# The chunk inverses of a gated DeltaNet in two 16-row blocks instead of one 32-row loop

## The chip, the cores and the metric

The kernel runs on one core of one Trainium2 chip. The metric is the device time of one execution in microseconds (us). An engine's instructions run in the order that was fixed when the program was built: a scheduler places every instruction of TensorE (PE), VectorE (DVE), ScalarE (ACT), GpSimd (POOL) and the DMA queue of SyncE (SP) by a simulated timeline, and each engine then takes its own list from the top, waiting at each instruction for what it needs.

## The reference

Two layers of a hybrid encoder on 512 tokens of width 1024. A layer has a mixer (a gated MLP, a sliding-window attention and a bidirectional gated DeltaNet, each on its own columns of one projection), then 16 experts and an input gate. The part that matters here is the DeltaNet, cut from the reference:

```python
lower = jnp.where(strict, jnp.einsum('bhntd,bhnsd->bhnts', k_beta, kc) * decay, 0.0)
eye = jnp.eye(C, dtype=F32)
t_inv = lax.linalg.triangular_solve(lower + eye, jnp.broadcast_to(eye, lower.shape),
                                    left_side=True, lower=True, unit_diagonal=True)
u = t_inv @ (vc * bc[..., None])
w = t_inv @ (k_beta * jnp.exp(gc)[..., None])
...
def step(state, inp):
    v_new = u_n - w_n @ state
    o_n = (q_n * jnp.exp(g_n)[..., None]) @ state + qk_n @ v_new
    ...
o_f = gated_delta_chunked(q, k, v, g[0], beta[0])
o_b = flip(gated_delta_chunked(flip(q), flip(k), flip(v), flip(g[1]), flip(beta[1])))
```

For every head, chunk and direction, a unit lower triangular matrix has to be inverted before the scan over the chunks can start.

## The kernel before

The kernel cuts the tokens into 16 chunks of 32 (6 heads, 2 directions: 192 matrices of 32x32; on the tiles the four chunks of a token tile lie in the four groups of 32 partitions, with 24 matrices of each direction in the free dimension; the chunk length changes nothing in the result). A mixer runs in this order of code: the norm, the gated MLP, the decays, the DeltaNet's projections, `gdn_chunk` (the matrices `AT`, from the products pG, L867), `gdn_inv` (L875), the MLP's output, `attn_qk` (L464), `gdn_inv_T` (L897), and then the scan (`gdn_scan`, L907) with its fill work between the steps (the attention's values vp, its core, the first part of the output projection). The scheduler moves work of these parts past each other.

`gdn_inv` inverts on VectorE. AT is transposed so that each matrix lies within a partition (X, 1024 elements a direction), multiplied by minus the betas (L887), and then inverted in place by 30 steps of forward substitution; step j multiplies a column by a row (L892, into T) and adds the product (L894), both directions at once. `gdn_inv_T` transposes X back into XT (L903) and scales it by the betas (L904). The scan's first product, pV (L943, 12 products of 32x32 by 32x64 a step), reads XT.

`attn_qk` has three projection blocks (0, 1, 2) of 256 columns of queries and keys. For each it runs 96 products (name qkp, lines L340 to L342 of a helper: high by high, low by high, high by low), squares on ScalarE for the norms, a reciprocal square root by Newton steps on VectorE (L175 to L182, 13 small operations), a scaling on POOL (L522, four operations), the rotary products on VectorE (L527, four or eight, then L529 and L530), and transposes on TensorE (qkTp, L496), whose copies ScalarE makes (L501, L502, L504). The high halves of the weights are made by ScalarE (L330, whi) and the low halves by POOL (L332, wlo), 512 elements a piece for these blocks and 384 for the attention's values.

The transposes of a block and the copies of the block before are interleaved in the code: after each token tile of block i comes one tile of block i-1.

Tiles come from pools: `slot` has 12 buffers of 128x2048, `gslot` two (X and XT take them here), PSUM's `pg` four.

Of the kernel before, what the change touches and what calls it, by code (L numbers as in the profile page):

```python
# [14 lines left out]
AF = mybir.ActivationFunctionType  # L15
ALU = mybir.AluOpType
# [93 lines left out]
class K:  # L110
# [428 lines left out]
    def gmlp(self, l, w):  # L539
# [12 lines left out]
        for t in range(NT):  # L552
# [6 lines left out]
            v.scalar_tensor_tensor(uv[:, t, :], x2, 1.0, p, op0=ALU.add, op1=ALU.mult)  # L559
            v.tensor_reduce(mu[:, t, :], vv[:, t], axis=AX.X, op=ALU.add)  # L560
            v.tensor_scalar(mu[:, t, :], mu[:, t, :], 1.0 / 64, None, op0=ALU.mult)
            v.tensor_tensor(vv[:, t], vv[:, t], mu[:, t, :, None].to_broadcast([128, 4, 64]), op=ALU.subtract)
            sq = self.p1([128, 4, 64], "sqv")
            act.activation(sq, vv[:, t], AF.Square)
            v.tensor_reduce(var[:, t, :], sq, axis=AX.X, op=ALU.add)
        f = lambda a: a.rearrange("p t g -> p (t g)")
# [308 lines left out]
    def gdn_inv(self, l):  # L875
        self.mark("inv")
        nc, mp = self.nc, self.mp
        v, act, pe, pool_e = nc.vector, nc.scalar, nc.tensor, nc.gpsimd
        br, AT = self.br, self.AT
        brT = self.small([128, 2, 32], "brT")  # L880
        v.transpose(brT, br)
        v.tensor_scalar(brT, brT, -1.0, None, op0=ALU.mult)
        X = self.gslot("X").rearrange("p (c i j) -> p c i j", c=2, i=32)
        for dr in range(2):
            Xd = X[:, dr] if dr == 0 else X[:, dr].rearrange("p i j -> p j i")
            v.transpose(Xd, AT[:, dr].rearrange("p m b -> p b m"))
            v.tensor_tensor(Xd, Xd, brT[:, dr, :, None].to_broadcast([128, 32, 32]), op=ALU.mult)  # L887
        pool_e.memset(X.rearrange("p c i j -> p c (i j)")[:, :, ::33], 1.0)
        for j in range(1, 31):
            n = 31 - j  # L890
            T = self.t(3, [128, 2, n, j], "T")
            v.tensor_tensor(T, X[:, :, j + 1:, j:j + 1].to_broadcast([128, 2, n, j]),  # L892
                            X[:, :, j:j + 1, 0:j].to_broadcast([128, 2, n, j]), op=ALU.mult)
            v.tensor_tensor(X[:, :, j + 1:, 0:j], X[:, :, j + 1:, 0:j], T, op=ALU.add)  # L894
        self.X = X

    def gdn_inv_T(self, l):  # L897
        self.mark("invT")
        v, pe, br, X = self.nc.vector, self.nc.tensor, self.br, self.X
        XT = self.XT = self.gslot("XT").rearrange("p (d m b) -> p d m b", d=2, m=32)  # L900
        for dr in range(2):
            Xd = X[:, dr] if dr == 0 else X[:, dr].rearrange("p i j -> p j i")
            v.transpose(XT[:, dr].rearrange("p m t -> p t m"), Xd)  # L903
        v.tensor_tensor(XT[:, :, 0:24], XT[:, :, 0:24], br[:, :, 0:24, None].to_broadcast([128, 2, 24, 32]), op=ALU.mult)  # L904


    def gdn_scan(self, l):  # L907
        nc, mp = self.nc, self.mp
        v, act, pe, pool_e = nc.vector, nc.scalar, nc.tensor, nc.gpsimd
        KQT, XT, QKm, kdec, vtok, EG, DC = self.KQT, self.XT, self.QKm, self.kdec, self.vtok, self.EG, self.DC  # L910
        o_sum = self.o_sum = self.gslot("o_sum")[:, :NT * 384].rearrange("p (t n) -> p t n", t=NT)
# [3 lines left out]
        for n in range(NCH):  # L915
# [25 lines left out]
            for h in range(6):  # L941
                for dr, ch, cc, tl in cur:
                    pe.matmul(pV[kl[dr], h, :], XT[kl[dr], dr, 6 * tl + h, :],  # L943
                              rhs[dr][:, h * 64:(h + 1) * 64], start=True, stop=True)
# [552 lines left out]
```

## Time and profile before

| | us |
|---|---|
| median of 3 runs | 1959.53 (1959.13 to 1962.07) |
| the profiled execution | 1958.17 |
| its span, first to last instruction | 1956.2 |
| TensorE busy | 1799.0 (92%) |
| VectorE busy | 930.7 (48%) |
| ScalarE busy | 523.6 (27%) |
| POOL busy | 457.6 (23%) |

The profile is of one execution. Of its span, the inversion in the first layer runs from 168 to 228 us and in the second from some 1130 to 1192; the experts fill most of the rest. Times below are us from the start of the span. A float32 product of TensorE stands in the trace as two records, so a pV of 12 products is "x24". Busy time of TensorE counts overlapping products once.

### The profile page before, as it was taken

The page shows a single profiled execution, that of the slowest core. Times are in us where ns is not written, and L with a number is a line of the kernel's source. Part 1 is how long each engine was busy: PE and PEld are TensorE (multiplying, and loading weights), DVE is VectorE, ACT ScalarE, POOL GpSimd, SP SyncE. Part 2 cuts the span into 40 slices and gives each one's busy share as a digit, 9 for nine tenths or more (in the row PEclk, how much of TensorE's full clock was granted, in tenths as well). Part 3 has the DMA queues.
Part 4 walks back from the last instruction along what each step waited for, and adds up shares of the span by engine and source line. Part 5 has one row for each costly group of instructions (what it writes and reads, how often), then busy time and mean ns, then how long its engine had stood idle before and what let it go on. Part 6 is the DMA issues. An engine that isn't in the chain of part 4 may idle for free.

```text
span 1956.2 us, 30065 instructions
## 1 busy us (share of the span) xinstructions
PE 1799.0 (92%) x12216; PEld 1126.8 (58%) x12216; DVE 930.7 (48%) x2088; ACT 523.6 (27%) x1213; POOL 457.6 (23%) x402
## 2 busy tenths in 40 slices
PE   5898698979999999999988978899799999999998
PEld 5777665864434444335987767568544343443368
DVE  5879868661211111422788896786511212114135
ACT  4334444231111101102443344452211010011032
POOL 3544413420000003201645352233100000022033
PEclk9989889989999999999998978899799999999999
DMA  5212020287899999999242020204798999999981
GB/s 169 87 34 60 17 85 16 109 321 296 347 412 412 390 412 411 366 414 374 85 131 82 21 71 24 76 2 168 305 356 345 412 406 395 415 372 393 414 289 65
DMA packets 168730, 467.46 MB, mean 239 GB/s; under 512 B 11664, under 2 KB 68496, under 8 KB 168592
## 3 DMA queue, kind: packets, MB, share of 16 engines
q1 hardware_dynamic: 161504, 458.46, 61.0%
q10 hardware_dynamic: 7088, 7.09, 1.2%
q8 instruction: 96, 1.57, 0.3%
q14 instruction: 42, 0.34, 0.1%
HBM read 461.32 MB, written 4.19 MB: 238 GB/s over the span
## 4 chain that ended last, share of the span: by engine, by line
PE 68%; DVE 21%; ACT 4%; issue 3%; POOL 2%; DMA 2%; SPq 1%; ACTq 0%; DVEq 0%; POOLq 0%
PE pGt L1270 15%; PE pUp L1270 11%; PE pY L1270 10%; DVE acc L770 3%; PE xep L1198 2%; DVE rr L936 2%; PE ysc L1289 2%; PE xep L1199 2%; PE op L340 1%; PE ysc L1290 1%; PE pV L943 1%; PE plep L1164 1%; PE pgp L342 1%; PE pgp L340 1%; PE pY L1385 1%
## 5 line engine op out<-in xcount | busy, mean ns | idle before, releaser
L1270 PE MATMUL pUp<-w,xe 128*64 128x512 f32 x800 | 200.8, 595 | 0.0
L1270 PE MATMUL pGt<-w,xe 128*64 128x512 f32 x640 | 200.4, 600 | 0.0
L332 POOL TENSOR_TENSOR wlo<-w,whi 128x512 fp32r<-128x512 f32 (+5 forms) x66 | 161.3, 2463 | 114.7 <-ACT whi L330 99.9
L1270 PE MATMUL pY<-w,hidT 128*64 128x512 f32 x720 | 186.9, 596 | 0.0
L1337 POOL TENSOR_TENSOR x<-x,hh 128x1024 f32<-128x1024 f32 x8 | 18.9, 2358 | 615.5 <-DVE x L1295 615.4
L1270 PEld LDWEIGHTS pUp<-w,xe 128*64 128x64 f32 x800 | 70.7, 137 | 101.8 <-issue 98.0
L1295 DVE TENSOR_TENSOR x<-ysc,x 128x512 f32<-128x512 f32 x96 | 63.2, 686 | 117.9 <-PE ysc L1290 117.9
L1270 PEld LDWEIGHTS pGt<-w,xe 128*64 128x64 f32 x640 | 58.6, 136 | 99.7 <-issue 97.6
L1270 PEld LDWEIGHTS pY<-w,hidT 128*64 128x64 f32 x720 | 64.1, 136 | 89.9 <-issue 87.4
L1270 PE MATMUL pGt<-wx,xe 128*64 128x512 f32 x320 | 114.4, 603 | 0.3
L1328 DVE SCALAR_TENSOR_TENSOR hid<-sg,gsl,pUp 128x512 f32<-128x512 f32 x32 | 23.7, 747 | 159.7 <-PE pUp L1270 158.1
L1354 DVE SCALAR_TENSOR_TENSOR yl<-pY,gsl,yh 128x512 fp32r<-128x512 f32 x28 | 21.0, 751 | 165.2 <-ACT yh L1353 163.7
L1321 DVE SCALAR_TENSOR_TENSOR sg<-sg,pGt 128x512 f32<-128x512 f32 x32 | 21.8, 686 | 132.2 <-ACT sg L1320 132.2
L330 ACT ACTIVATE whi<-w 128x512 fp32r<-128x512 f32 (+5 forms) x66 | 68.0, 1058 | 38.5 <-PE op L341 15.8
L342 PE MATMUL pgp<-whi,gTl 128*128 128x256 f32 x256 | 72.8, 292 | 3.9 <-DVE gTl L271 3.9
L329 POOL TENSOR_TENSOR w<-w,pp 128x512 f32<-128x512 f32 x32 | 32.4, 1047 | 179.2 <-DMA w<-in_w_ple_gate_dram 107.7
L1320 ACT ACTIVATE sg<-pGt,gsl 128x512 f32<-128x512 f32 x32 | 21.8, 687 | 192.2 <-PE pGt L1270 190.2
L340 PE MATMUL pgp<-whi,gTh 128*128 128x256 f32 x256 | 73.0, 289 | 0.0
L1200 ACT ACTIVATE xe<-xep,pp 128x256 f32<-128x256 f32 x64 | 30.2, 474 | 158.7 <-PE xep L1199 158.7
L341 PE MATMUL pgp<-wlo,gTh 128*128 128x256 f32 x256 | 72.4, 288 | 0.0
L1198 PE MATMUL xep<-OH,hh 128*128 128x256 f32 x256 | 69.1, 304 | 2.5 <-DVE OH L1186 2.5
L1344 ACT ACTIVATE hidT<-htp 128x512 f32<-128x512 f32 x32 | 19.1, 597 | 193.5 <-PE htp L1343 193.5
(404 smaller groups left out, 4277.0 us busy)
## 6 DMA issues: line engine op xcount, KB each, us to landing
w<-in_w_e_up_dram SPq DMA_DIRECT2D x100, 1024.0 KB, 14.6
w<-in_w_e_down_dram SPq DMA_DIRECT2D x90, 1024.0 KB, 11.3
w<-in_w_e_gate_dram SPq DMA_DIRECT2D x80, 1024.0 KB, 12.9
wx<-in_w_e_gate_dram SPq DMA_DIRECT2D x40, 1024.0 KB, 11.6
wx<-in_w_e_up_dram SPq DMA_DIRECT2D x28, 1024.0 KB, 12.2
wx<-in_w_e_down_dram SPq DMA_DIRECT2D x22, 1024.0 KB, 8.3
wd<-in_w_e_down_dram SPq DMA_DIRECT2D x32, 512.0 KB, 8.8
w<-in_w_in_dram SPq DMA_DIRECT2D x14, 1024.0 KB, 5.0
```

What stands on the lines that cost most here:

```text
L330: self.nc.scalar.activation(rr_(hi[:, ks, :]), wk, AF.Copy)
L332: e.tensor_tensor(rr_(lo[:, ks, :]), wk, hi[:, ks, :], op=ALU.subtract)
L340: pe.matmul(p, lh, rh, start=first, stop=False)
L341: pe.matmul(p, lh, rl, start=False, stop=False)
L342: pe.matmul(p, ll, rh, start=False, stop=last)
L770: v.scalar_tensor_tensor(acc, raw[:, kk:kk + S], conv[:, b, kk:kk + 1], acc, op0=ALU.mult, op1=ALU.add)
L936: v.tensor_tensor(rr[kl[dr], :], vtok[kl[dr], tl, :], fl(tm[kl[dr]]), op=ALU.subtract)
L1198: pe.matmul(p, rr_(hh[:, t, ks]), OHf[:, t, :], start=(t == 0), stop=False)
L1199: pe.matmul(p, rr_(hl[:, t, ks]), OHf[:, t, :], start=False, stop=(t == NT - 1))
L1270: pe.matmul(pt[nh][64 * ei:64 * ei + 64, :], lhs[:, kk, 64 * ei:64 * ei + 64], wt[ei][k][:, nh * 512:nh * 512 + 512], start=(kk == 0), sto ...
L1289: pe.matmul(p, rr_(OT[:, t, :]), rr_(yh[:, ns]), start=True, stop=False)
L1295: v.tensor_tensor(xv, p, xv, op=ALU.add)
```

## The change

X keeps its place, but only its two 16x16 diagonal blocks are inverted by VectorE: they are taken into a buffer XN (four blocks: two directions by two), and a loop of 14 steps inverts all four at once. ScalarE copies the inverted blocks into X, whose other two quadrants POOL has set to zero. In `gdn_inv_T`, XN is then used again for X transposed the other way; TensorE multiplies the block of AT between the two diagonal blocks by one inverse (pY1), VectorE scales that by the betas into a buffer Y, TensorE multiplies it by the other inverse (pY2), and VectorE subtracts the result from XT and scales XT by the betas, each direction by itself. Each of pY1 and pY2 is 192 products of 32x32 by 32x16 a layer.

```diff
         X = self.gslot("X").rearrange("p (c i j) -> p c i j", c=2, i=32)
+        XN = self.XN = self.slot("XN")
+        B = XN[:, 0:1024].rearrange("p (c e i j) -> p c e i j", c=2, e=2, i=16)
         for dr in range(2):
             Xd = X[:, dr] if dr == 0 else X[:, dr].rearrange("p i j -> p j i")
             v.transpose(Xd, AT[:, dr].rearrange("p m b -> p b m"))
-            v.tensor_tensor(Xd, Xd, brT[:, dr, :, None].to_broadcast([128, 32, 32]), op=ALU.mult)
-        pool_e.memset(X.rearrange("p c i j -> p c (i j)")[:, :, ::33], 1.0)
-        for j in range(1, 31):
-            n = 31 - j
-            T = self.t(3, [128, 2, n, j], "T")
...
+            for i in range(2):
+                s = slice(16 * i, 16 * i + 16)
+                Bd = B[:, dr, i] if dr == 0 else B[:, dr, i].rearrange("p i j -> p j i")
+                v.tensor_tensor(Bd, Xd[:, s, s], brT[:, dr, s, None].to_broadcast([128, 16, 16]), op=ALU.mult)
+        Bf = B.rearrange("p c e i j -> p (c e) i j")
+        pool_e.memset(Bf.rearrange("p c i j -> p c (i j)")[:, :, ::17], 1.0)
+        pool_e.memset(X[:, :, 0:16, 16:32], 0.0)
+        pool_e.memset(X[:, :, 16:32, 0:16], 0.0)
+        for j in range(1, 15):
+            n = 15 - j
+            T = self.t(3, [128, 4, n, j], "T")
+            v.tensor_tensor(T, Bf[:, :, j + 1:, j:j + 1].to_broadcast([128, 4, n, j]),
+                            Bf[:, :, j:j + 1, 0:j].to_broadcast([128, 4, n, j]), op=ALU.mult)
+            v.tensor_tensor(Bf[:, :, j + 1:, 0:j], Bf[:, :, j + 1:, 0:j], T, op=ALU.add)
+        for i in range(2):
+            s = slice(16 * i, 16 * i + 16)
+            act.activation(X[:, :, s, s], B[:, :, i], AF.Copy)
...
         XT = self.XT = self.gslot("XT").rearrange("p (d m b) -> p d m b", d=2, m=32)
+        XN = self.XN.rearrange("p (d m b) -> p d m b", d=2, m=32)
+        Y = self.slot("Y").rearrange("p (d m b) -> p d m b", d=2, m=32)
+        cs = [(slice(0, 16), slice(16, 32)), (slice(16, 32), slice(0, 16))]
         for dr in range(2):
+            nc.gpsimd.memset(Y[:, dr, 0:24, cs[dr][1]], 0.0)
+        for dr in range(2):
+            v.transpose(flip(XN[:, dr]), flip(X[:, dr]) if dr == 0 else X[:, dr])
+        for dr in range(2):
+            p = self.pg([128, 24, 16], "pY1")
+            for m in range(24):
+                for r in rows:
+                    pe.matmul(p[r, m, :], AT[r, dr, m, :], XN[r, dr, m, cs[dr][0]], start=True, stop=True)
+            v.tensor_tensor(Y[:, dr, 0:24, cs[dr][0]], p, br[:, dr, 0:24, None].to_broadcast([128, 24, 16]), op=ALU.mult)
+        for dr in range(2):
+            v.transpose(flip(XT[:, dr]), X[:, dr] if dr == 0 else flip(X[:, dr]))
+        for dr in range(2):
+            p = self.pg([128, 24, 16], "pY2")
+            for m in range(24):
+                for r in rows:
+                    pe.matmul(p[r, m, :], Y[r, dr, m, :], XT[r, dr, m, cs[dr][1]], start=True, stop=True)
+            xo = XT[:, dr, 0:24, cs[dr][1]]
+            v.tensor_tensor(xo, xo, p, op=ALU.subtract)
+            xd = XT[:, dr, 0:24]
+            v.tensor_tensor(xd, xd, br[:, dr, 0:24, None].to_broadcast([128, 24, 32]), op=ALU.mult)
-            Xd = X[:, dr] if dr == 0 else X[:, dr].rearrange("p i j -> p j i")
-            v.transpose(XT[:, dr].rearrange("p m t -> p t m"), Xd)
-        v.tensor_tensor(XT[:, :, 0:24], XT[:, :, 0:24], br[:, :, 0:24, None].to_broadcast([128, 2, 24, 32]), op=ALU.mult)
```

In the changed kernel the lines are: the loop L901 and L903, ScalarE's copies L906, XN's transposes L924, pY1's products L929, Y's scaling L930, XT's transposes L932, pY2's products L937, the subtraction L939, the scaling L941, and pV L980. The lists below name the buffers of pY1 pY_2097 (first direction) and pY_2195 (second), and those of pY2 pY_2295 and pY_2394.

The lists of the engines change order as well, in both layers alike. On TensorE, in the changed kernel, the products qkp of block 1 are interrupted after 47 of its 96 (the rest of the 96 follow):

```order
L342 MATMUL qkp<-whi,xl 128x256
L340 MATMUL qkp<-whi,xh 128x256
L341 MATMUL qkp<-wlo,xh 128x256
L342 MATMUL qkp<-whi,xl 128x256
L929 MATMUL pY_2097<-XN,AT 32x16 x14
L340 MATMUL qkp<-whi,xh 128x256
L341 MATMUL qkp<-wlo,xh 128x256
L342 MATMUL qkp<-whi,xl 128x256
L340 MATMUL qkp<-whi,xh 128x256
```

Before, nothing stood between these products; now 14 of pY1 do, so what follows on TensorE waits for the first of XN's transposes. pY1 goes on in 12 more pieces through block 2, up to a last one of 87.

On TensorE at the first block's transposes, before (the products here belong to block 2):

```order
L340 MATMUL qkp<-whi,xh 128x256
L341 MATMUL qkp<-wlo,xh 128x256
L342 MATMUL qkp<-whi,xl 128x256
L496 MATMUL qkTp<-cst,qk 128x128 x4
L340 MATMUL qkp<-whi,xh 128x256
L341 MATMUL qkp<-wlo,xh 128x256
L342 MATMUL qkp<-whi,xl 128x256
L340 MATMUL qkp<-whi,xh 128x256
```

and in the changed kernel, where block 2's first product is the last L340 shown:

```order
L342 MATMUL qkp<-whi,xl 128x256
L340 MATMUL qkp<-whi,xh 128x256
L929 MATMUL pY_2097<-XN,AT 32x16 x14
L496 MATMUL qkTp<-cst,qk 128x128 x2
L929 MATMUL pY_2097<-XN,AT 32x16 x21
L496 MATMUL qkTp<-cst,qk 128x128 x2
L929 MATMUL pY_2097<-XN,AT 32x16 x6
L340 MATMUL qkp<-whi,xh 128x256
```

Here 41 products of pY1 stand in three pieces around four transposes, ahead of block 2's first product. Before, block 0's first transposes came behind block 2's 23rd product; now its first four stand 11 products ahead of block 1's end, and the others follow as shown.

On VectorE, the end of the inversion, before (L529 and L530 are block 1's, L175 is block 2's):

```order
L529 TENSOR_TENSOR qk<-ro 128x16x8
L530 TENSOR_TENSOR qk<-ro 128x16x8
L892 TENSOR_TENSOR T<-X 128x60
L894 TENSOR_TENSOR X<-X,T 128x2x30
L903 STREAM_TRANSPOSE XT<-X 128x32x32 x2
L904 TENSOR_TENSOR XT<-XT,br 128x2x768
L175 TENSOR_SCALAR nr<-ssq 128x16
```

and in the changed kernel (L175 to L182, L527 to L530 all of block 2):

```order
L930 TENSOR_TENSOR Y<-pY_2097,br 128x24x16
L175 TENSOR_SCALAR nr<-ssq 128x16
L930 TENSOR_TENSOR Y<-pY_2195,br 128x24x16
L176 TENSOR_SCALAR nr<-nr 128x16
L177 TENSOR_SCALAR nr<-nr 128x16
L932 STREAM_TRANSPOSE XT<-X 128x32x32 x2
...
L181 TENSOR_TENSOR nr<-nr 128x16
L182 SCALAR_TENSOR_TENSOR ra<-nr,ra 128x16
L939 TENSOR_TENSOR XT<-XT,pY_2295 128x24x16
L941 TENSOR_TENSOR XT<-XT,br 128x768
L527 TENSOR_TENSOR ro<-qk,rot 128x128 x4
L529 TENSOR_TENSOR qk<-ro 128x16x8
L530 TENSOR_TENSOR qk<-ro 128x16x8
L939 TENSOR_TENSOR XT<-XT,pY_2394 128x24x16
L941 TENSOR_TENSOR XT<-XT,br 128x768
```

L175 of block 2 moved ahead of the transposes into XT, and block 2's rotary (L527 to L530) ahead of the last subtraction and scaling of XT; before, it came behind pV.

On POOL, the changed kernel has the order: four low halves of block 1, block 0's scaling, four low halves of block 2, Y's two memsets, block 1's scaling, four low halves of the values, block 2's scaling, the last four low halves. Before, the eight low halves of blocks 1 and 2 came ahead of block 0's scaling, and block 2's scaling came last. On ScalarE, L906 stands behind the first high half of block 2, and the others behind L906. SP's order is unchanged. The second V weights' low half takes Y's slot, and so waits for pY2.

## Rows read from the trace of the kernel before

**Rows 1.** The page: busy time by engine, and the chain that ended last by engine.
```profile
PE 1799.0 (92%) x12216; PEld 1126.8 (58%) x12216; DVE 930.7 (48%) x2088; ACT 523.6 (27%) x1213; POOL 457.6 (23%) x402
...
PE 68%; DVE 21%; ACT 4%; issue 3%; POOL 2%; DMA 2%; SPq 1%; ACTq 0%; DVEq 0%; POOLq 0%
```

**Rows 2.** Windows: stretch, its us, busy us by engine, granted clock, DMA share, GB/s.
```profile
182.50:196.00 13.50, 12.88 (x107) 12.68 (x105) 13.40 (x26) 9.24 (x43) 7.00 (x5) 0.99 0.42 114
196.00:207.00 11.00, 0.55 (x5) 0.37 (x4) 10.39 (x17) 0.33 (x3) 7.90 (x8) 0.67 0.24 59
440.00:450.00 10.00, 9.86 (x51) 5.02 (x51) 0.00 (x0) 1.85 (x4) 0.00 (x0) 0.89 0.38 131
```

**Rows 3.** Chain of waits, 178 to 235 us: start, us, what.
```profile
189.50 8.01 issue
...
201.53 4.06 DVE ro L527 x4
```

**Rows 4.** Groups by line, VectorE, 150 to 240 us: busy us, mean ns | idle before.
```profile
L892 DVE TENSOR_TENSOR T<-X 128x60 f32<-128x60 f32 (+14 forms) x30 | 23.4, 781 | 0.4
L894 DVE TENSOR_TENSOR X<-X,T 128x60 f32<-128x60 f32 (+14 forms) x30 | 18.7, 623 | 0.4
...
L903 DVE STREAM_TRANSPOSE XT<-X 128x1024 f32<-128x1024 f32 x2 | 4.2, 2164 | 0.0
L887 DVE TENSOR_TENSOR X<-X,brT 128x1024 f32<-128x1024 f32 x2 | 3.4, 1724 | 0.0
```

**Rows 5.** Timeline, VectorE: start, us, instruction [idle before <-releaser].
```profile
168.34 0.25 DVE L892 TENSOR_TENSOR T<-X 128x60 f32<-128x60 f32 x1
...
178.28 5.37 DVE L892 TENSOR_TENSOR T<-X 128x368 f32<-128x368 f32 x1
...
197.41 0.66 DVE L892 TENSOR_TENSOR T<-X 128x480 f32<-128x480 f32 x1
...
233.84 1.50 DVE L527 TENSOR_TENSOR ro<-qk,rot 128x128 f32<-128x128 f32 x4 [0.76 <-POOL qk L522]
```

**Rows 6.** Timeline, POOL, 170 to 240 us.
```profile
178.28 11.22 POOL L332 TENSOR_TENSOR wlo<-wraw,whi 128x512 fp32r<-128x512 f32 x8
...
231.48 2.33 POOL L522 TENSOR_TENSOR qk<-qk,ra 128x256 f32<-128x256 f32 x4 [2.55 <-DVE ra L182]
```

**Rows 7.** Timeline, TensorE, first layer.
```profile
150.24 0.77 PE L867 MATMUL pG<-KQT 64*32 64x64 f32 x48
150.94 0.59 PE L850 MATMUL pD<-GC,mcst 128*128 128x192 f32 x2
...
206.70 1.09 PE L496 MATMUL qkTp<-cst,qk 128*128 128x128 f32 x4 [10.46 <-DVE qk L530]
...
222.51 0.28 PE L341 MATMUL qkp<-wlo,xh 128*128 128x256 f32 x1
222.63 0.28 PE L342 MATMUL qkp<-whi,xl 128*128 128x256 f32 x1
...
228.13 0.86 PE L943 MATMUL pV<-vtok,XT 32*32 32x64 f32 x24 [0.80 <-DVE XT L904]
228.91 0.45 PE L340 MATMUL vp<-whi,xh 128*128 128x384 f32 x1
...
246.80 0.86 PE L943 MATMUL pV<-rr,XT 32*32 32x64 f32 x24
...
255.08 0.85 PE L943 MATMUL pV<-rr,XT 32*32 32x64 f32 x22 [0.22 <-DVE rr L936]
```

**Rows 8.** Timeline, ScalarE: what follows the last square of block 2.
```profile
225.73 0.35 ACT L501 ACTIVATE att<-qkTp,gT 64x128 f32<-64x128 f32 x1
```

**Rows 9.** Timeline, TensorE, second layer: first and third pV.
```profile
1192.17 0.86 PE L943 MATMUL pV<-vtok,XT 32*32 32x64 f32 x24 [0.85 <-DVE XT L904]
...
1213.06 0.86 PE L943 MATMUL pV<-rr,XT 32*32 32x64 f32 x24
```

**Rows 10.** Loads of the experts' first weights (L1258): durations, first and last issue.
```profile
L1258 SPq DMA_DIRECT2D wx<-in_w_e_gate_dram x3: 410/440/850, 375.9 to 376.9; - x3
```

More of the change, by code (lines that the diff above doesn't have):

```diff
@@ L886, in gdn_inv @@
             v.transpose(Xd, AT[:, dr].rearrange("p m b -> p b m"))
-            v.tensor_tensor(Xd, Xd, brT[:, dr, :, None].to_broadcast([128, 32, 32]), op=ALU.mult)
-        pool_e.memset(X.rearrange("p c i j -> p c (i j)")[:, :, ::33], 1.0)
-        for j in range(1, 31):
-            n = 31 - j
-            T = self.t(3, [128, 2, n, j], "T")
-            v.tensor_tensor(T, X[:, :, j + 1:, j:j + 1].to_broadcast([128, 2, n, j]),
-                            X[:, :, j:j + 1, 0:j].to_broadcast([128, 2, n, j]), op=ALU.mult)
-            v.tensor_tensor(X[:, :, j + 1:, 0:j], X[:, :, j + 1:, 0:j], T, op=ALU.add)
+            for i in range(2):
[15 more added lines that the diff above has]
+            act.activation(X[:, :, s, s], B[:, :, i], AF.Copy)
         self.X = X
@@ L898, in gdn_inv_T @@
         self.mark("invT")
-        v, pe, br, X = self.nc.vector, self.nc.tensor, self.br, self.X
+        nc = self.nc
+        v, pe, br, X, AT = nc.vector, nc.tensor, self.br, self.X, self.AT
+        rows = [slice(32 * c, 32 * c + 32) for c in range(4)]
         XT = self.XT = self.gslot("XT").rearrange("p (d m b) -> p d m b", d=2, m=32)
+        XN = self.XN.rearrange("p (d m b) -> p d m b", d=2, m=32)
+        Y = self.slot("Y").rearrange("p (d m b) -> p d m b", d=2, m=32)
+        cs = [(slice(0, 16), slice(16, 32)), (slice(16, 32), slice(0, 16))]
         for dr in range(2):
-            Xd = X[:, dr] if dr == 0 else X[:, dr].rearrange("p i j -> p j i")
-            v.transpose(XT[:, dr].rearrange("p m t -> p t m"), Xd)
-        v.tensor_tensor(XT[:, :, 0:24], XT[:, :, 0:24], br[:, :, 0:24, None].to_broadcast([128, 2, 24, 32]), op=ALU.mult)
+            nc.gpsimd.memset(Y[:, dr, 0:24, cs[dr][1]], 0.0)
+        flip = lambda a: a.rearrange("p i j -> p j i")
+        for dr in range(2):
[17 more added lines that the diff above has]
+            v.tensor_tensor(xd, xd, br[:, dr, 0:24, None].to_broadcast([128, 24, 32]), op=ALU.mult)
     def gdn_scan(self, l):
```

## The prediction

> **What bounds the kernel now.** I read the page first: TensorE is busy 92% of the span and holds 68% of the chain that ended last, VectorE 48% and 21% [rows 1]. That average says nothing of the stage around the change, so next come the windows there: from 182.5 to 196 us TensorE, VectorE and ScalarE all work, then from 196 to 207 TensorE is busy 0.55 of 11 us and VectorE 10.4 [rows 2]. The chain says why: 8.01 us as "issue", in which it waits for nothing that the profile shows, and, after POOL's scaling, 4.06 us for the four rotary products (L527) of the first projection block, block 0 [rows 3]. All of that block's chain queues on VectorE among the steps of the loop, and TensorE's first four transposes sit 10.46 us idle for it [rows 7]. At the stage's end the first pV, with which the scan starts, waits 0.80 us for XT's scaling (L904) [rows 7]. So VectorE bounds this stretch in both places, and the loop is what fills it: L892 and L894 take 23.4 + 18.7 = 42.1 us in 60 operations, the two transposes into XT 4.2 [rows 4].
>
> **The change, part by part (first layer, in the times of the trace before).** I follow it to the first pV, at 228.13 before, since nothing of the change lies behind it.
>
> 1. *The products into X.* Two of 1024 (3.4 us [rows 4]) become four of 256. An operation costs about 0.19 us and 0.98 ns an element (60 elements 0.25, 480 elements 0.66 [rows 5]), so 4 x 0.44 = 1.8: the loop can start 1.1 to 1.6 earlier than 168.34; I take 167.2.
> 2. *The loop.* 60 operations become 28 with 2 x 2240 = 4480 elements: 28 x 0.19 + 4480 x 0.98 ns = 9.7, about 10 us for 42.1. But other work of VectorE stands among its steps, as before, and one operation froze for 5.37 us while POOL made low halves from 178.28 on [rows 5, 6]. POOL's order still has four of them there; I let the loop be two thirds done, freeze 5.2, and end at 187.0.
> 3. *XN.* ScalarE copies the two diagonal blocks (L906, 512 elements each, about 0.6 each: 1.2), and VectorE transposes twice at 2.1 (L924; L903's row is 2 in 4.2 [rows 4]): 192.6. The first pY needs the first transpose: 190.5. TensorE has only 47 of block 1's 96 products ahead of it (done near 186.3) and idles some 4 us behind it, which is paid from the 10.46 it idled anyway.
> 4. *Block 0's rotary.* Behind XN on VectorE: five small operations 1.0, POOL's scaling 2.4 (2.33 [rows 6]), L527 4.06 again, since POOL makes four low halves beside it as before, and 0.5: first transposes at 200.6, against 206.70.
> 5. *TensorE to the end of block 2.* From 200.6: 106 products at 0.12 [rows 7] are 12.7; 12 transposes at 0.2 (four in 1.09 at the low clock [rows 2, 7]) 2.4; and 70 pY products. Nothing of 32x16 is in the trace. The nearest rows are pG, 24 products (48 records, two for each float32 product) in 0.70, and pV, 12 products (24 records) in 0.78, each to the next start [rows 7]: 0.03 and 0.065 a product, switches to and from the big products included. pY's four quadrants are more like pG's four column groups, but in eight short pieces, each with its own switches: 0.04, so 2.8. One more for a clock that falls in the waits (0.67 in the idle window [rows 2]). End of block 2: 219.5, against 222.75.
> 6. *Block 2's squares.* Before, the last ended at 225.73, where the next copy starts [rows 8], 3 us after the block. Now the last token tile's squares stand on ScalarE behind copies of two more pairs of transposes, with 19 pY products before those: I take 5. 224.4.
> 7. *The tail on VectorE.* Here the order is worse than before. It puts L175 (which waits for those squares) ahead of the second L930, of both transposes into XT and of L939. So from 224.4: L175, L930 and two small ones 1.0, XT 4.2, ten small ones 2.1; L939 and L941 of the first direction; then block 2's whole rotary, which before came after the first pV (233.84 [rows 5]), and only then L939 and L941 of the second direction, which pV needs. POOL's scaling 2.4 covers the first pair; L527 takes 4.06, because POOL's next work is four low halves, where before it was 1.50 [rows 5]; then 0.5, and L939 + L941 (384 and 768 elements) 0.55 + 0.9. Sum: 15.7, first pV at 240.1: **12.0 later than before.** The 192 pY products of the second kind (5.8 at 0.03) and 87 of the first lie under these steps.
> 8. *What the scan gives back.* From the first to the third pV before took 18.67 and, in the second layer, 20.89 [rows 7, 9], with block 2's rotary in between; a step without it takes 8.28 [rows 7], two 16.6. So 2.1 and 4.3 come back: +9.9 and +7.7, together +17.5.
>
> POOL's memsets of X's and Y's zero blocks (four of 512 or 384 elements) lie in its waits; if they didn't, 0.5 each. SP's order is unchanged. The second V weights' low half takes Y's slot, so waits for the last pY; its first user stands behind pV anyway.
>
> 1958.17 (span 1956.2 and 1.97 outside it) + 17.5 = 1975.7, **1976**. The median of the runs shown lies 1.36 above the profiled execution, which I don't add.
>
> **Bounds.** Low: no freeze in the loop (-4.8), both rotaries at 1.50 (-5.1), products at 0.03 (-0.7): first pV near 229.5, the scan gives back its 2 to 4, and the time is about 1956. High: products at 0.065 put 1.8 on TensorE before block 2's end, and 12.5 instead of 5.8 for the second kind, of which about 1 shows; L522 at twice its 2.33, as when POOL and VectorE run together, 2 more each time: some +6 a layer, 1988 to 1990.
>
> **The rivals.**
> - *A. VectorE was the bound and is free; TensorE now sets the start of the scan: faster.* For it: 32 us of work leave VectorE. From 186.3 TensorE owes 144 products x 0.12 = 17.3, 18 transposes 3.6, 384 pY products 11.5 to 25, 18 vp 3.2: 36 to 49, a pV at 222 to 235 if it never waited. It decides if the first pV comes before about 230 (what the scan gives back). At 223 to 225, 4 us earlier, and with 1 or so of what the scan gives back, the time is 1958 - 2 x 5 = about 1948. Against it: waits of TensorE at the first pY, at block 0's transposes and for block 2's rotary, all fixed by the order.
> - *B. No change: the delay is absorbed later.* If the experts' first weights set when the experts start, the mixer could shift freely: 1959. Against: their loads are issued at 375.9, and when the experts start (440 to 450) DMA is busy 0.38 only [rows 10, 2]. The scan would have to hide 12 us behind its fill work, but it is itself the chain.
> - *C. Each switch between small and big products drains TensorE.* If each waits out a product in flight (0.28 for the big one [rows 7]), eight pieces are 16 switches, 4.5, with 70 products at 0.015 each 1.0: 5.5 for the 2.8 I took, +2.7 a layer and up to 1 more at pY's last pieces: about 1982. The row speaks against the full price: pV's 24 records are busy for 0.86 us, and the next big product starts 0.78 after the first of them [rows 7], before the last is out. [...]
>
> **How the numbers follow.** My forecast 0.57, C 0.17, A 0.17, B 0.09. The range, 1956 to 1990, holds the forecast with its bounds, B and C; A's 1948 is outside. This kernel's runs tell 0.2% (3.9 us) from no change. Faster: A, 0.17. Same: B and the forecast's lowest end, 0.09. Slower: 0.74.
>
> **What would show it.** In the changed profile: the loop (now L901 and L903) in 28 operations near 10 us plus one freeze; the first pY near 190.5 with TensorE idle before it; the first transposes of block 0 near 200.6; block 2's last product near 219.5; block 2's L527 *before* the first pV, that one near 240, waiting for VectorE's L941. A first pV before 230 proves me wrong in 5 to 7; a pV at 240 with a time below 1965 proves me wrong in 8; pieces of pY that cost much more or less than 0.04 a product show which bound of 5 holds.

## The result, and the profile after

The changed kernel took 1981.29 us (median of 7 runs, 1974.05 to 1987.44), the kernel before, on the same chip, 1962.07 (7 runs, 1959.13 to 1970.03). The ratio is 1.0075, 95% interval 1.0054 to 1.0095: slower, by 14.7 us (the two medians lie 19.2 apart; the seven runs of each kernel scatter over 11 and 13 us). The profiled execution of the changed kernel took 1974.52, its span is 1972.6, 16.4 above the span before; 17.5 was forecast. The number was right, but three of its eight steps (4, 7 and 8) were wrong, in directions that cancel, and a cost of the products had not been seen. The page of the changed kernel, its parts 1 and 3 (queue, packets, MB, share):

```profile
PE 1828.9 (93%) x13752; PEld 1144.9 (58%) x13752; DVE 890.0 (45%) x2042; ACT 526.2 (27%) x1217; POOL 456.2 (23%) x410
...
q8 instruction: 108, 1.77, 0.4%
```

VectorE lost 41 us of busy time against [rows 1], TensorE gained 30 and 1536 records: 768 a layer, two for each of the 384 small products. The queue that brings instructions had 96 packets before and has 108. This line was on the page of before too, and the prediction did not look at it.

Now the stage in the first layer. TensorE's timeline (start, duration, idle time before it and what ended it), to be read beside [rows 7]:

```profile
188.25 0.61 PE L929 MATMUL pY<-XN,AT 32*32 32x16 f32 x28 [4.78 <-DVE XN L924]
...
195.62 0.60 PE L496 MATMUL qkTp<-cst,qk 128*128 128x128 f32 x4
...
206.49 0.28 PE L342 MATMUL qkp<-whi,xl 128*128 128x256 f32 x1
206.70 0.43 PE L929 MATMUL pY<-XN,AT 32*32 32x16 f32 x30
207.06 0.38 PE L340 MATMUL qkp<-whi,xh 128*128 128x256 f32 x1
207.28 0.28 PE L341 MATMUL qkp<-wlo,xh 128*128 128x256 f32 x1
207.40 0.28 PE L342 MATMUL qkp<-whi,xl 128*128 128x256 f32 x1
...
209.91 0.28 PE L342 MATMUL qkp<-whi,xl 128*128 128x256 f32 x1
210.12 0.23 PE L929 MATMUL pY<-XN,AT 32*32 32x16 f32 x2
...
210.62 0.28 PE L342 MATMUL qkp<-whi,xl 128*128 128x256 f32 x1
...
213.56 0.28 PE L342 MATMUL qkp<-whi,xl 128*128 128x256 f32 x1
...
221.16 1.41 PE L937 MATMUL pY<-XT,Y 32*32 32x16 f32 x146 [0.85 <-DVE XT L932]
224.90 1.91 PE L937 MATMUL pY<-XT,Y 32*32 32x16 f32 x128 [2.33 <-issue]
228.35 1.69 PE L937 MATMUL pY<-XT,Y 32*32 32x16 f32 x110 [1.55 <-issue]
...
231.34 0.69 PE L341 MATMUL vp<-wlo,xh 128*128 128x384 f32 x1 [0.68 <-POOL wlo L332]
...
233.96 1.49 PE L980 MATMUL pV<-vtok,XT 32*32 32x64 f32 x24
```

The 4.78 us before the first pY were forecast. The three rows at L937 are not what was forecast: the 384 records follow each other every 8.5 ns at first (146 in 1.41 us, where the piece of 30 above took 0.43), but they come in three runs, with 2.33 and 1.55 us between them in which TensorE waits for nothing that the profile shows, and the second run is exactly 128 records long. In the second layer they come in runs of 256 and 128, with one such gap, of 1.90 us. VectorE's timeline in the same stretch:

```profile
174.98 5.38 DVE L901 TENSOR_TENSOR T<-XN 128x216 f32<-128x216 f32 x1
...
186.23 3.80 DVE L924 STREAM_TRANSPOSE XN<-X 128x1024 f32<-128x1024 f32 x2 [0.41 <-ACT X L906]
...
193.40 0.90 DVE L527 TENSOR_TENSOR ro<-qk,rot 128x128 f32<-128x128 f32 x4 [2.51 <-POOL qk L522]
...
218.38 0.26 DVE L175 TENSOR_SCALAR nr<-ssq 128x16 f32<-128x16 f32 x1 [3.64 <-ACT sqa L516]
...
219.17 3.79 DVE L932 STREAM_TRANSPOSE XT<-X 128x1024 f32<-128x1024 f32 x2
...
228.01 0.90 DVE L527 TENSOR_TENSOR ro<-qk,rot 128x128 f32<-128x128 f32 x4 [0.50 <-POOL qk L522]
...
230.10 0.56 DVE L939 TENSOR_TENSOR XT<-XT,pY 128x384 f32<-128x384 f32 x1 [0.66 <-PE pY L937]
230.69 1.42 DVE L941 TENSOR_TENSOR XT<-XT,br 128x768 f32<-128x768 f32 x1
```

One operation of the loop still froze (5.38, where the sum of as many elements behind it took 0.38), but the rotaries of blocks 0 and 2 took 0.90 each, not 4.06 [rows 3]. POOL's timeline shows what stood beside them:

```profile
175.14 4.98 POOL L332 TENSOR_TENSOR wlo<-wraw,whi 128x512 fp32r<-128x512 f32 x4
...
197.52 4.98 POOL L332 TENSOR_TENSOR wlo<-wraw,whi 128x512 fp32r<-128x512 f32 x4 [4.16 <-ACT att L502]
...
230.29 4.59 POOL L332 TENSOR_TENSOR wlo<-wraw,whi 128x384 fp32r<-128x384 f32 x4 [2.31 <-PE pY L937]
```

The low halves that should have stood beside block 0's rotary waited 4.16 us for ScalarE, and the last ones until the last pY freed Y's buffer, so neither met a rotary. Before, four low halves stood beside the 4.06, which began at 201.53:

```profile
201.46 3.98 POOL L332 TENSOR_TENSOR wlo<-wraw,whi 128x384 fp32r<-128x384 f32 x4
```

And the windows of the scan's first two steps, from the first pV to the second and on to the third (busy time of PE, PEld, DVE, ACT, POOL, then the granted clock, DMA share, GB/s):

```profile
233.90:246.50 12.60, 12.52 (x125) 10.93 (x125) 3.02 (x8) 2.83 (x9) 1.81 (x3) 0.59 0.01 1
246.50:255.80 9.30, 9.07 (x128) 7.83 (x128) 3.89 (x9) 2.10 (x7) 0.83 (x1) 1.00 0.01 2
```

TensorE is busy throughout both (12.52 of 12.60 us and 9.07 of 9.30), but the first runs at a granted clock of 0.50 up to 244 us and takes 12.6 us; before it took 9.1 in this layer (79.8 - 70.7 after the inverse's start, in the count of the next table).

Since stages start at different times, what follows counts "after A": from the start of the two transposes of AT with which the inverses begin (157.46 before, 155.92 now). First layer and second:

| | before | changed | forecast (first layer) |
|---|---|---|---|
| first qkTp | 49.2, 49.8 | 39.7, 39.8 | 43.1 |
| first pV | 70.7, 70.7 | 78.0, 75.3 | 82.6 |
| third pV | 89.3, 91.6 | 99.9, 97.9 | 99.2 |

The two third pVs are late by 10.6 + 6.3 = 16.9 us, and the span grew by 16.4. What lies outside these stretches nearly cancels: A comes 1.5 us earlier in the first layer, and 0.3 and 0.8 are added behind the two third pVs.

### The profile page after: what moved, and what is told of

It reads as the page before. It is cut to its first block, busy times and chain, and to the rows that moved or that the text cites. A ratio compares the mean times of both kernels' runs of the same rounds, so it can differ in the third digit from the quotient of the medians.

```text
span 1972.6 us, 33111 instructions
## 1 busy us (share of the span) xinstructions
PE 1828.9 (93%) x13752; PEld 1144.9 (58%) x13752; DVE 890.0 (45%) x2042; ACT 526.2 (27%) x1217; POOL 456.2 (23%) x410
## 5 line engine op out<-in xcount | busy, mean ns | idle before, releaser
L1307 PE MATMUL pY<-w,hidT 128*64 128x512 f32 x720 | 191.9, 599 | 0.0
L1374 POOL TENSOR_TENSOR x<-x,hh 128x1024 f32<-128x1024 f32 x8 | 18.9, 2358 | 622.6 <-DVE x L1332 622.5
L1307 PEld LDWEIGHTS pY<-w,hidT 128*64 128x64 f32 x720 | 65.7, 137 | 92.0 <-issue 89.3
L1307 PEld LDWEIGHTS pGt<-w,xe 128*64 128x64 f32 x640 | 58.5, 136 | 99.9 <-issue 97.8
L329 POOL TENSOR_TENSOR w<-w,pp 128x512 f32<-128x512 f32 x32 | 32.3, 1044 | 177.7 <-DMA w<-in_w_ple_gate_dram 106.0
L340 PE MATMUL pgp<-whi,gTh 128*128 128x256 f32 x256 | 71.5, 283 | 0.0
## 6 DMA issues: line engine op xcount, KB each, us to landing
w<-in_w_e_gate_dram SPq DMA_DIRECT2D x80, 1024.0 KB, 12.6
wx<-in_w_e_up_dram SPq DMA_DIRECT2D x28, 1024.0 KB, 11.6
```

The source lines that it names most:

```text
L329: self.nc.gpsimd.tensor_tensor(wk, wk, gain[:, ks, None].to_broadcast([128, step, cols]), op=ALU.mult)
L340: pe.matmul(p, lh, rh, start=first, stop=False)
L1307: pe.matmul(pt[nh][64 * ei:64 * ei + 64, :], lhs[:, kk, 64 * ei:64 * ei + 64], wt[ei][k][:, nh * 512:nh * 512 + 512], start=(kk == 0), sto ...
```

## The experiments

**The theory after the result**: VectorE's shorter loop is worth much, TensorE's 384 small products take it back, because TensorE gets their instructions too slowly. **The rivals**: the order of the tail on VectorE (step 7) holds the first pV; each change between small and big products costs the time of a big product (rival C); the products' columns cost.

*1. Without the products.* Both sets, XN's second use, Y and the subtraction are left out, so the block between the two inverses stays zero; loop, copies and XT's scaling stay, in the changed kernel's own place.

```diff
-            v.transpose(flip(XN[:, dr]), flip(X[:, dr]) if dr == 0 else X[:, dr])
...
-                    pe.matmul(p[r, m, :], AT[r, dr, m, :], XN[r, dr, m, cs[dr][0]], start=True, stop=True)
...
-                    pe.matmul(p[r, m, :], Y[r, dr, m, :], XT[r, dr, m, cs[dr][1]], start=True, stop=True)
```

> Leaves out both sets of small products with what serves them (XN's second use, Y, the subtraction): the block between the two 16x16 blocks of each inverse is left at zero. It shows what the shorter loop alone is worth. Theory (the loop was on the path of block 0's rotary and of XT; what made the change slower came behind it): XT is ready some 30 us earlier than before, TensorE then sets the first pV, near 213 in the first layer (228.13 before), the scan gives some of it back, and the time is 1930 to 1940. Rival (VectorE's loop was never on the path): first pV no earlier than 224 and a time within 6 us of 1959.

Measured: 1940.55, ratio 0.9875 (0.9844 to 0.9907), instruction packets 96; first pV 64.7 and 62.0 after A. The time lies 0.6 us above the theory's range and far below the rival's; the pV comes 5.9 and 8.7 earlier than before, where some 15 were expected. So the loop's part of the change is worth 24.5 us (1.25% of 1963; 18 to 31 by the interval, and 14.9 between the spans of the two traces), and its second part costs about 39 (31 between the spans).

*2. The tail in another place.* `gdn_inv_T` is called inside the projections, ahead of block 2, with its steps unchanged.

```diff
-            self.gdn_inv_T(l)
...
-            first(i, self.wnext(small=True) if i else wq)
+            w = self.wnext(small=True) if i else wq
+            if i == 2:
+                self.gdn_inv_T(l)
+                self.mark("attn_qk")
+            first(i, w)
```

> The same instructions as the change; only the code of gdn_inv_T is put ahead of the third projection block, so that its products, XT's transposes, the subtraction and the scaling take their places ahead of block 2's squares and rotary. Theory (the order of the tail made the change slower: XT's last steps queue behind block 2's squares and rotary): the first pV waits for TensorE alone, comes near 225 instead of 233.96 in the first layer, block 2's rotary falls behind it again, and the time is 1950 to 1964. Rival (the 384 small products a layer, with the fetching of their instructions, cost the 16 us wherever they stand): no better than 1970.

Measured: 1971.3, ratio 1.0035 (1.0021 to 1.0049), first pV 78.2 and 78.7. The rival held: the order gives back 8 us (0.40%; 5.2 between the spans), yet the first pV does not come earlier, because TensorE now sets it: it works without a wait from the end of the second products to the pV. Its timeline:

```profile
212.38 2.21 PE L940 MATMUL pY<-XT,Y 32*32 32x16 f32 x237
216.93 1.90 PE L940 MATMUL pY<-XT,Y 32*32 32x16 f32 x128 [2.34 <-issue]
220.38 0.50 PE L940 MATMUL pY<-XT,Y 32*32 32x16 f32 x19 [1.55 <-issue]
```

The same gaps, again 128 records apart, and here one of 2.11 in pY1 as well. What the order gave back came from the scan: from the first to the third pV took 18.7 in both layers, where the changed kernel took 21.9 and 22.5. The first step ran at full clock:

```profile
235.40:243.40 8.00, 7.64 (x122) 6.52 (x122) 5.37 (x21) 2.25 (x11) 4.35 (x7) 1.00 0.01 3
```

*3. The same with XT's transposes first and Y in XN's buffer*, so that the values' low halves don't wait for Y.

```diff
-        Y = self.slot("Y").rearrange("p (d m b) -> p d m b", d=2, m=32)
+        Y = XN
...
+        for dr in range(2):
+            v.transpose(flip(XT[:, dr]), X[:, dr] if dr == 0 else flip(X[:, dr]))
+        for dr in range(2):
+            nc.gpsimd.memset(Y[:, dr, 0:24, cs[dr][1]], 0.0)
         for dr in range(2):
             p = self.pg([128, 24, 16], "pY1")
...
-        for dr in range(2):
-            v.transpose(flip(XT[:, dr]), X[:, dr] if dr == 0 else flip(X[:, dr]))
```

> As the run with gdn_inv_T ahead of block 2, and besides: XT's transposes directly behind XN's, and Y kept in XN's buffer, so that the values' low halves don't wait for the second products. Theory: two waits that the profile of the change shows go (0.85 us of TensorE for XT's transposes, 2.31 us of POOL for the second products, which TensorE's vp then waits 1.0 for), so 1 to 3 us a layer under the run beside it. Rival (TensorE is busy there anyway): within 2 us of the run beside it.

Measured: 1976.9, ratio 1.0061 (1.0038 to 1.0083), first pV 78.3 and 78.5 as in 2. No gain in the stage; the 5 us more lie outside it (AT's transposes start 4 us later already), and why stays open.

*4. Every small product issued twice*, in the changed kernel's own place.

```diff
                     pe.matmul(p[r, m, :], AT[r, dr, m, :], XN[r, dr, m, cs[dr][0]], start=True, stop=True)
+                    pe.matmul(p[r, m, :], AT[r, dr, m, :], XN[r, dr, m, cs[dr][0]], start=True, stop=True)
...
+                    pe.matmul(p[r, m, :], Y[r, dr, m, :], XT[r, dr, m, cs[dr][1]], start=True, stop=True)
                     pe.matmul(p[r, m, :], Y[r, dr, m, :], XT[r, dr, m, cs[dr][1]], start=True, stop=True)
```

> Every small product is issued twice, with the same result. It prices them. Theory (a product costs some 20 ns, and more where instructions run short, and lies on the path where TensorE is waited for): the second products, 8.8 us long in the profile of the change with 3.9 us of that idle, take about twice that, the pieces in block 2 add 1.4; +6 to +11 us a layer, 1987 to 1997. Rival (what costs is the switching between small and big products, of which there are no more than before): +2 us a layer at most, under 1980.

Measured: 2021.4, ratio 1.0289 (1.0265 to 1.0313), first pV 99.2 and 99.8: 21 to 24 us a layer for 768 records more, 28 to 32 ns each, where records at speed are 8.5 apart. All expectations were far too low. The waits of TensorE from 185 to 256 us (total, times, longest), the instruction queue, and what DMA moved from 236 to 256 in slices of 0.5 us:

```profile
PE pY L939 <- issue: 7.7, 4, 2.3
PE pY L930 <- issue: 5.7, 3, 2.1
```

```profile
q8 instruction: 120, 1.97, 0.4%
...
GB/s 0 33 0 0 0 0 0 0 0 33 0 0 0 0 0 0 33 0 0 0 0 0 0 0 33 0 0 0 0 0 0 0 33 0 0 0 0 0 0 0
```

Nothing else uses DMA there, and one instruction packet of 16 KB (1.97 MB in 120) comes about every 3.9 us. Over all runs the packets follow the records exactly: 96 with 12216, 102 with 12984, 108 with 13752, 120 with 15288, so one for 128 records, each a weight load and a product. 3.9 us for 128 is 30 ns a record, which is the price measured. This run made the supply the leading theory.

*5. The products in eight portions*, after the token tiles of blocks 1 and 2, so that the supply has time.

```diff
+            inv = self.gdn_inv_T(l)
+            next(inv)
+            self.inv = inv
...
+                if (i, t) >= (1, 1):
+                    next(self.inv, None)
...
+                yield
```

> The same instructions as the run with gdn_inv_T ahead of block 2, but the small products are written out in eight portions of 48, one behind each token tile of blocks 1 and 2, so that big products stand between most of them. Counted from the start of the transposes of AT, the first pV came at 78.2 us there (70.7 before the change), and TensorE stood idle within the small products for 2.1 + 3.9 us in gaps 128 records apart. Theory (TensorE's instructions arrive in blocks at some 3.5 us each, too slowly for a run of small products, which use up 4 instructions a product): most of the 6 us goes, first pV at 71 to 74, time 1954 to 1964. Rival (small products cost what they cost, and each switch to and from them costs more): more pieces, first pV at 78 or later, 1970 or more.

Measured: 1974.18, ratio 1.0052 (1.0031 to 1.0073). The theory's range for the time is missed, and the rival's is met. The gaps are gone (none in either layer), and block 2 ends at 68.6 instead of 74.9, though half of the second products, 186 records in one piece and 6 before it, now stand behind it; but the first pV still stands at 76.8 and 77.2. The waits of TensorE from 178 to 240:

```profile
PE qkTp L500 <- DVE qk L536: 3.3, 2, 2.5
...
PE vp L341 <- POOL wlo L332: 1.7, 2, 1.3
```

The time that the supply had cost went into waits for a rotary and for the values' weights, and the scan's first step ran at 0.71. So the gaps were not the sole hold in that order.

*6. Half of the work back to VectorE*: steps 1 to 15 of the loop on all 32 rows, the rest on the second block; only one set of products is left, in the place of 2. In the second direction this version multiplies the block between by the first inverse once more instead of by the second, so what it computes is not the reference's; its operations are as many and as large as the plan asks for. The edit is against the kernel before.

```diff
-        for j in range(1, 31):
+        for j in [*range(1, 16), *range(17, 31)]:
```

> VectorE's loop takes the first of the two products over: steps 1 to 15 of the old loop on all 32 rows (so that the lower block is multiplied by the first inverse), then steps 17 to 30 on the second diagonal block alone; TensorE does one set of 192 products a layer instead of two. The loop grows from 28 operations (near 10 us) to 58 with 12160 elements (near 23; before it was 42). gdn_inv_T stands ahead of block 2. Theory (TensorE and the supply of its instructions set the first pV, VectorE has time): first pV at 68 to 73 from the transposes of AT, 1948 to 1962. Rival (VectorE's loop is what counts, 13 us longer): block 0's transposes 13 us later and the first pV at 78 or later, 1968 or more.

Measured: 1976.15, ratio 1.0066 (1.0046 to 1.0086), first pV 77.1 and 81.2, 102 packets. The loop's products and sums take 34.1 us instead of 15.6, and TensorE waits for VectorE and for instructions both:

```profile
PE qkTp L495 <- DVE qk L529: 6.8, 1, 6.8
PE pY L928 <- issue: 4.5, 2, 2.4
```

The rival about held: at half the products, the longer loop costs more than they save.

*7. Products half as wide* (8 columns, half of the block between left out), otherwise as 2.

```diff
-        cs = [(slice(0, 16), slice(16, 32)), (slice(16, 32), slice(0, 16))]
+        cs = [(slice(0, 8), slice(16, 24)), (slice(16, 24), slice(0, 8))]
...
-            p = self.pg([128, 24, 16], "pY2")
+            p = self.pg([128, 24, 8], "pY2")
```

> As the run with gdn_inv_T ahead of block 2, with the small products 8 columns wide instead of 16 (half of the block between is left out): as many instructions, half the columns. Theory (instructions arrive too slowly): the second products still take 8 to 9 us from first to last with gaps of some 2 us, and the first pV stays at 77 to 79 from the transposes of AT. Rival (the columns are what takes the time): the second products take under 6 us, the first pV comes at 73 or earlier.

Measured: 1976.28 in its one run (2 had 1971.3), first pV 79.0 and 78.7, the second kind of product 9.4 us long with 4.62 of gaps, 8.5 and 3.89 in 2. One run says little of the time; the stretch says that columns are not the price.

*8. One wide product in place of 96 small ones*, otherwise as 2; the work of all other engines stays, and the values of the block between are not the reference's.

```diff
-            for m in range(24):
-                for r in rows:
-                    pe.matmul(p[r, m, :], Y[r, dr, m, :], XT[r, dr, m, cs[dr][1]], start=True, stop=True)
+            pe.matmul(p, Y[:, dr, 0:4, :].rearrange("p m b -> p (m b)"), XT[:, dr, 0:24, cs[dr][1]], start=True, stop=True)
```

> As the run with gdn_inv_T ahead of block 2, but each set of 96 small products of a direction is one product of 128x128 by 128x384 into the same tile (the block between is then not the reference's). All that the change adds on VectorE, ScalarE and POOL stays: the copies L906, XN's transposes, both scalings into Y, the subtraction, the scaling in two halves, and every wait between them. Theory (the 384 small products a layer and the supply of their instructions cost the change its gain): first pV at 62 to 68 from the transposes of AT, as without any products (64.7 and 62.0), and 1934 to 1946. Rival (the added steps on the other engines and the waits between them cost it): first pV at 73 or later, 1958 or more.

Measured: 1956.02, ratio 0.9959 (0.9938 to 0.998), first pV 69.0 and 68.7, no gap. Between both expectations. Against 2 it says that the small products with their supply cost 0.76%, 15 us (19.5 between the spans of the traces). Of the 9.2 and 10.0 us by which its first pV comes before that of 2, the gaps of 2 make up 6.0 and 6.7. Against 1 it says that the change's other steps, with the move ahead of block 2, cost 0.84%, 16.5 (6.6 between the spans); what the move alone does to a kernel without small products no run shows. A part of it is a rotary that froze again: 5.28 us, where it took 0.90 in 2. Its row on VectorE, and TensorE's wait for it:

```profile
193.73 5.28 DVE L526 TENSOR_TENSOR ro<-qk,rot 128x128 f32<-128x128 f32 x4 [2.50 <-POOL qk L521]
```

```profile
PE qkTp L495 <- DVE qk L529: 3.8, 1, 3.8
```

*9 and 10. The products in bfloat16*, one record each instead of two, with number, size and order kept: once in the place of 2, once in the changed kernel's own.

```diff
+            act.activation(ATb[:, dr], AT[:, dr, 0:24], AF.Copy)
...
+            act.activation(XTb[dr], XT[:, dr, 0:24, cs[dr][1]], AF.Copy)
...
-                    pe.matmul(p[r, m, :], Y[r, dr, m, :], XT[r, dr, m, cs[dr][1]], start=True, stop=True)
+                    pe.matmul(p[r, m, :], Y[r, dr, m, :], XTb[dr][r, m, :], start=True, stop=True)
```

> inv_T_before_block_2 (1.0035 of the kernel before) with the small products in bfloat16: ScalarE copies A, the diagonal inverses and the right-hand block to bfloat16 (six more operations, of 768 and 384 elements), VectorE writes Y as bfloat16, and each product is one record instead of two. Number, sizes and order of the products stay. Theory (TensorE is held by the supply of instructions): half the records are half the instructions, so the stretch of the second kind falls from 8.5 us to 4 to 5.5 and its idle time put down to issue from 3.9 us to 2 or less in the first layer; the first pV comes 72 to 75 us after AT's transposes instead of 78.2, and the time is 1955 to 1965, ratio 0.994 to 1.001. Rival (the cost belongs to each product: a change of the array's mode, an answer's latency): the second kind's stretch stays at 8 or more with its gaps, the first pV at 77 or later, the time at 1968 or above. Second rival (the scalar copies in the chain cost what the products save): the gaps go, but the first pV waits for ScalarE and comes at 77 or later.

> The changed kernel as it was predicted (its tail behind block 2's projection) with the products in bfloat16 in the same way. It measures step 7's claim, that the order of the tail holds the first pV, with the supply halved. If that order costs 8 us or more by itself: first pV 76 or later after AT's transposes in the first layer, the time 8 us or more above products_in_bf16. If TensorE's supply was all that mattered: first pV at 73 to 75, the time within 4 us of products_in_bf16.

Measured: 1966.57, ratio 1.0003 (0.9983 to 1.0024), in the place of 2; 1970.31, ratio 1.0032 (1.0013 to 1.0052), in the changed kernel's own. TensorE's timeline of the first:

```profile
206.06 1.73 PE L941 MATMUL pY<-XN,Y 32*32 32x16 bf16 x192
...
209.89 1.13 PE L950 MATMUL pY<-XT,Y 32*32 32x16 bf16 x96 [2.10 <-DVE ra L178]
...
214.29 0.30 PE L950 MATMUL pY<-XT,Y 32*32 32x16 bf16 x18 [2.02 <-issue]
...
230.63 0.86 PE L993 MATMUL pV<-vtok,XT 32*32 32x64 f32 x24
```

As the theory expected, the second kind takes 4.7 us instead of 8.5 with one gap of 2.02, the first pV stands at 73.6 and 72.8 instead of 78.2 and 78.7, and 6 us come back; the time is 1.6 us above the range given for it. The price follows the number of instructions (384 records of the second kind in 2, 192 here) and not that of products (192 in both). In the changed kernel's own place the pV stands at 77.3 and 71.4, and the two kernels differ by 3.7 us by their medians and 0.29%, 5.7 us, by their ratios: the order costs something by itself, less than the 8 us asked for, and the two layers disagree. The two layers of that one run also show the scan's first step at two granted clocks:

```profile
233.70:245.90 12.20, 12.16 (x125) 10.59 (x124) 2.98 (x8) 2.95 (x10) 0.83 (x1) 0.61 0.00 1
1202.60:1211.90 9.30, 8.97 (x128) 7.52 (x128) 5.04 (x17) 2.73 (x9) 3.16 (x5) 1.00 0.00 0
```

As many instructions of TensorE took 12.2 us at a clock of 0.61 and 9.3 at 1.00; in the first layer TensorE's long waits ahead of the first pV were for the values' weights (2.26 us) and for block 2's rotary (2.99).

No version that computes the block between by small products beat the kernel before; the best, 9, equals it, and rounds the factors to bfloat16.

## Why the prediction was right, and where it was not

In parts, by the ratios: the shorter loop gives back 24.5 us (1); the other steps that the change adds cost some 16.5 (8 against 1), the small products 15 (2 against 8), and the place of the tail 8 (the change against 2). That they add up to the measured time proves nothing, since each is the difference of two neighbours in one chain of runs, and by the intervals each is sure to some 5 to 8 us only. Counted by the third pV after A, both layers together and one trace of each kernel, the same parts are -15.1, +9.0, +19.5 and +3.5. The two counts differ on how the loss divides: by the traces the small products are by far its largest part, by the ratios they are no more than the other steps. The parts hold for this order of taking them: 1 keeps the changed kernel's place and 8 stands ahead of block 2, and 8's frozen rotary shows that they are not independent.

- *Steps 1 to 3* (loop, XN): right. The loop started 9.3 after A (forecast 9.7) and ended at 28.7 (29.5), its 28 operations took 15.6 with a freeze of 5.38 among them (10 and 5.2); the first pY came at 32.3 (33.0), with 4.78 of idle for "some 4".
- *Step 4* failed. "L527 4.06 again, since POOL makes four low halves beside it as before": it took 0.90, since POOL's next low halves waited 4.16 for ScalarE. The first transposes came 3.4 earlier than forecast.
- *Step 5*: right in sum, 18.2 us for 18.9. Its pieces are better resolved now. A piece of 2 records between big products delays these by 0.35 us, one of 14 by 0.43, one of 30 by 0.55 (206.49 to 207.40 and 209.91 to 210.62 above, less three big products at 0.12 each): about 0.33 for the two switches and 8 ns a record. The 1 us for the clock was not needed: it was granted at 1.00 from 195.6 to 213.8.
- *Step 6*: right, 4.5 for 5.
- *Step 7*: its sum was right by luck, 15.6 for 15.7 from L175 to the first pV; its terms were not. The rotary took 0.90 instead of 4.06; the second kind of product, which it took to be hidden at 5.8, took 8.9 and stood in the chain: L939 waited 0.93 and 0.66 for it, and POOL's low halves, then TensorE, waited for its end. The first pV did not wait for L941, as the forecast had it, but for TensorE's products for the values ahead of it (in the second layer 0.31 us for L941 within the pV). "Here the order is worse than before" is worth 8 us by 2 and 4 to 6 by 9 and 10: real, but the smaller part of the loss.
- *Step 8* failed, with the wrong sign. "So 2.1 and 4.3 come back": from first to third pV took 21.9 and 22.5, where before it took 18.7 and 20.9. Without block 2's rotary VectorE had 8 operations in the first step instead of 27, but TensorE ran it at a granted clock of 0.59, behind its waits. The step also misread the 20.9 as the rotary's: the first steps before (first layer, then second) had the rotary in both, as many instructions and a different clock, so of the 4.3 some 2.2 were the clock's.

```profile
228.20:237.30 9.10, 8.45 (x127) 7.18 (x128) 7.72 (x27) 4.00 (x14) 3.84 (x6) 1.00 0.01 2
1192.20:1203.80 11.60, 11.60 (x127) 10.02 (x127) 6.90 (x26) 3.35 (x11) 3.11 (x5) 0.71 0.01 1
```

So the first pV was forecast 12.0 late and came 7.4 and 4.6 late; the scan was to give back 2.1 and 4.3 and took 3.2 and 1.7 more. The errors of steps 4, 7 and 8 cancel to 1 us of 17.5. Steps 1 to 3, 5 and 6 held; that the time came out so close is luck.

*Rivals.* A's premise, that VectorE's free time is worth much, is shown by 1 (a time of 1940.55, where A gave 1948), and that TensorE then sets the scan's start, by 2; it failed on the price of the products, for which it allowed 11.5 to 25 us but no wait. B: nothing was absorbed. C: the switch is there, about 0.17 for each, not 0.28; block 2's 70 products cost 18.2 - 12.7 - 2.4 = 3.1 at the prediction's prices for the rest, of which C wanted 5.5 and the forecast 2.8 plus 1 for the clock. No row stood behind C's 0.015 a product; at speed its two records took 17 ns here.

## What to carry to other kernels

A product of 32x32 by 32x16 took TensorE 17 ns here at speed (two records of 8.5 at a granted clock of 1.00), and each record stands for two instructions, a weight load and a product (13752 of each in the changed kernel): before work is moved to TensorE as hundreds of small products, count their instructions beside the instruction queue's line of the page (here a packet for 128 records), and price a dense run by the supply (28 to 32 ns a record in 4), not by the pace between two gaps (8.5). Work of VectorE that is replaced must be weighed against all the steps around the replacement: here those other steps alone took back some six tenths of the gain by the traces (9.0 of 15.1) and two thirds by the ratios. Where an operation of VectorE froze in the first layer of the two kernels (5.37 and 4.06 before, 5.38 in the changed kernel's loop), POOL made low halves beside it, and the rotary of the 4.06 took 0.90 where it made none; so a forecast that keeps such a freeze must first say where that neighbour's work will stand.

## What the runs showed of the hardware that was not expected

- **The supply of instructions.** Dense small products followed each other every 8.5 ns at a granted clock of 1.00 and then stopped for 1.5 to 2.3 us, 128 records apart. One 16 KB packet of the instruction queue went with 128 records (12 packets more for 1536 records more), and in 4 one came every 3.9 us. Half the records (9) left 4.7 us of a stretch of 8.5. In 4 TensorE's waits put down to issue came to 7.7 and 5.7 us between 185 and 256. Why a packet takes so long to follow the last (the queue's packets fill 1.8% of DMA's time from 236 to 256 in 4, and nothing else uses it) stays open.
- **The clock after waits.** The scan's first step took 12.2 to 13.2 us where the granted clock was 0.59 to 0.61, and 8.0 to 9.4, with other work between its products, where it was 1.00. The kernel before shows it too: 9.1 at 1.00 in its first layer, 11.6 at 0.71 in its second. In two traces the clock fell after TensorE's waits, whether for instructions (the changed kernel: 1.00 from 221 to 223 us, 0.50 from 225 to 231, with the gap of 2.33 between) or for weights and VectorE (10: 1.00 from 212 to 218, 0.66 from 222 to 228, 0.50 from 233.7 to 240, with waits of 2.26 and 2.99 ahead of the last).
- **Small among big products.** In the changed kernel a piece of two records delayed the big products around it by 0.35 us (210.12), some twenty times the 17 ns that two records take at their own pace.
